# Norms by a power of -1/2 on POOL in place of ScalarE square roots and VectorE reciprocals: one step of an RWKV-7 / attention backbone

## The chip, the core and the metric

The kernel runs on one NeuronCore of a Trainium2 chip. The metric is the device time of one execution, in microseconds. The engines are named as in the profile: PE (TensorE), DVE (VectorE), ACT (ScalarE), POOL (GpSimd) and SP (SyncE, which issues all the DMAs here).

## The reference

One inference step of a model of two layers, for 256 context tokens and 1024 latent tokens of width 1024, all in float32. Layer 0 is bidirectional RWKV-7 time mixing beside a gated short convolution, layer 1 is grouped-query attention with 16 query and 4 key/value heads of 64. The norms are what matters for the change; there are five kinds:

```python
def rmsnorm(x, g):                       # rows of 1024 before each layer and at the end;
    xf = x.astype(f32)                   # heads of 64 for q and k
    y = xf * lax.rsqrt(jnp.mean(xf * xf, axis=-1, keepdims=True) + EPS)      # EPS = 1e-6
    return (y * g.astype(f32)).astype(x.dtype)

# layer 0, before the scan: keys to length one, per head of 64
kk = kk / jnp.maximum(jnp.sqrt(jnp.sum(kk * kk, axis=-1, keepdims=True)), 1e-12)
S_f, y_f = rwkv_scan(S0[:, 0], r_h, w_h[:, :, 0], k_h[:, :, 0], v_h, kk, a_h[:, :, 0], False)
S_b, y_b = rwkv_scan(S0[:, 1], r_h, w_h[:, :, 1], k_h[:, :, 1], v_h, kk, a_h[:, :, 1], True)
y = y_f + y_b
# layer 0, after the scan: group norm per head of 64
var = jnp.mean(jnp.square(y - mean), axis=-1, keepdims=True)
y = ((y - mean) * lax.rsqrt(var + GN_EPS)).reshape(B, L, A_WIDTH) * lnx_g + lnx_b   # GN_EPS = 64e-5
```

## The kernel before

**Order of the work.** Every stage is written as Python generators that yield what they need next (an engine and tiles) and then emit instructions. The class `Loom` is a planner: `issued` (lines 256 to 303) keeps a modelled clock for each engine, with the prices of `COST` (line 39), 6.25 ns per column for a reciprocal, and 1.28 us whenever ScalarE goes from one group of `TABLES` (line 46) to another; `run` (from line 327) always lets go on the generator that this model says can start in time, by the ranks of `PRECEDENCE`. What is emitted stands in program order on each engine, so a changed price or a changed engine gives all later work a new order. `pick` gives some additions to POOL or DVE, whichever the model has free first. The model knows no contention between DVE and POOL.

**Stages.** Start (0 to 60 us): rows of x are read, squared and summed on ACT, normed (`norm_x`), transposed and modulated, while the adaLN weights stream in. Even layer (to about 1170 us): `fill` runs the input projection, three fp32r products for each tile (high and low halves, `whi`, `wlo`, split from `wraw`), into which the scan is woven: 20 chunks for each of four pairs of heads, with products into the PSUM banks `wk`, `iv`, `ch`, `py`, triangular inverses of many small DVE operations on `acc` and `tmp`, and state steps in which POOL multiplies `hv` by the decay into `hg` and DVE adds it to PE's `ch`. Then the output projection, `rsqrt_mean` for each block of rows and the transposes for layer 1 (to about 1306), the odd layer's projections with the per-head norms (to about 1520), attention (to about 2140), the last products with `to_y`, which norms a block of rows and stores it.

**The norms.** All are Sqrt on ACT and RECIPROCAL on DVE:

- `norm_k` (from line 709): 20 groups of 128x256. ACT squares into `sq` (one buffer, `bufs=1`), PE sums each head by a product with `ones2` into a `wk` bank, ACT takes the root out of the bank, DVE takes the maximum with 1e-12 and the reciprocal, and one DVE operation scales the keys; a store follows on SP.
- `close_groups` (from line 1239): 20 groups of 128x256 in `sqy` (one buffer), root with scale 1/64 and bias `GN_EPS`, reciprocal on DVE, product with `y` on POOL, two DVE operations with the gates, a store.
- `norm_x` (from line 1296): three calls with 4, 2 and 4 columns.
- `rsqrt_mean` (line 1747): one column, for each of ten blocks of rows in both layers.
- `normed_heads` (line 1839): 4 or 8 columns, 30 times.

Tanh and Exp are the functions used most on ACT; Silu runs twice at the start.

Of the kernel before, what the change touches and what calls it, by code (L numbers as in the profile page):

```python
# [12 lines left out]
ALU = mybir.AluOpType  # L13
# [26 lines left out]
BIAS = {"V": 0.3, "sum": 3.0}  # L40


WINDOW = 3.413


TABLES = {AF.Tanh: 0, AF.Exp: 0, AF.Sqrt: 1, AF.Silu: 2}

PRECEDENCE = (("loaded", -0.1), ("bonuses", 0), ("h0", 0.3), ("chained", 0), ("moved", 0.3), ("tailed0", 0),
              ("evac", -0.1), ("h1", 1.0), ("x", -0.1), ("interacted", 0), ("solved1", 0), ("solved", 0),
# [67 lines left out]
class Loom:  # L117
# [128 lines left out]
    def issued(self, e, name, a, k, r):  # L246
        if not self.on:
            return
        args = list(a) + list(k.values())
        aps = [x for x in args if isinstance(x, bass.AP)]  # L250
        outs = [k["out"]] if "out" in k else aps[:1]
        if k.get("accum_out") is not None:
            outs.append(k["accum_out"])
        ins = [x for x in aps if not any(x is o for o in outs)]
        n = (ins if name == "tensor_reduce" else outs)[0].free_size()
        if e == "T":
            group = None
            if name == "transpose":
                dur = 0.107
            else:  # L260
                dur = max(0.054, n * (1 if ins[0].dtype == F32R else 4) / 2400.0)
                if ins[0].dtype == F32R and ins[0].partition_size() == 64:

                    group = ("rows", ins[0].start_partition() if callable(ins[0].start_partition) else ins[0].start_partition)
                    if self.last is not None and group != self.last:
                        dur, group = 0.014, None
                elif ins[0].free_size() <= 64:
                    group = outs[0].start_partition() if callable(outs[0].start_partition) else outs[0].start_partition
                    if self.last is not None and group != self.last:
                        dur, group = 0.053, None  # L270
            self.last = group
        elif e == "V":
            dur = COST[e][0] + n * (6.25e-3 if name == "reciprocal" else COST[e][1])
            if isinstance(k.get("scalar"), bass.AP):
                dur += 0.065
        elif e == "S":
            dur = COST[e][0] + n * COST[e][1] + 0.14 * isinstance(k.get("scale"), bass.AP) \
                + 0.09 * isinstance(k.get("bias"), bass.AP)
            f = a[2] if len(a) > 2 else None
            if f in TABLES and TABLES[f] != self.table:  # L280
                self.table = TABLES[f]
                dur += 1.28
        elif e == "G":
            dur = COST[e][0] + n * COST[e][1]
        items = [self.item(x, False) for x in ins] + [self.item(x, True) for x in outs]
        start = max([self.clock[e]] + [self.free(e, x) for x in items])
        if e == "T":
            dur = self.paced(start, dur, P if ins[0].dtype == F32R else ins[0].partition_size())
        if e == "D":
            self.clock[e] = start + 0.475  # L290
            piece = min(x.ap[-1][1] if x.ap[-1][0] == 1 else 1 for x in outs + ins)
            self.moved = max(self.moved, start + 1.1) + outs[0].nbytes() / (360e3 if piece >= 128 else 180e3)
            end = self.moved + 0.86
        else:
            self.clock[e] = end = start + dur
        for x in items:
            self.note(e, x, end)
        self.tc.keep_in_program_order(r)
        self.trace.append((r.ins.name, start, end))
# [68 lines left out]
def hybrid_step(  # L368
# [31 lines left out]
    V.memset(ones2[0:64, 0:64], 1.0)  # L400
    V.memset(ones2[64:128, 64:128], 1.0)
    eps_t = const.tile([P, 2], F32, name="eps_t")
    V.memset(eps_t[:, 0:1], EPS)
    V.memset(eps_t[:, 1:2], GN_EPS)


    rows = {}
# [307 lines left out]
    def norm_k(p, b, f, done):  # L715

        t0, n, _ = BLK[b]
        for h in range(0, n, GRP):
            fh = f[:, h:h + GRP]
            yield "S", fh  # L720
            sq = ip.tile([P, GRP], F32, tag="sq", name="sq", bufs=1)
            S.activation(sq, fh, AF.Square, scale=col("k_k", p))
            yield "T", sq, wk_ps
            pt = wk_ps.take()
            T.matmul(pt[:, 0:GRP], ones2, sq, start=True, stop=True)
            yield "S", pt
            S.activation(sq, pt[:, 0:GRP], AF.Sqrt)
            wk_ps.release(pt)
            yield "V", sq
            V.tensor_scalar(out=sq, in0=sq, scalar1=1e-12, scalar2=None, op0=ALU.max)  # L730
            yield "V", sq, 1.7
            V.reciprocal(out=sq, in_=sq)
            yield "V", sq, Into(fh)
            V.scalar_tensor_tensor(out=fh, in0=fh, scalar=col("k_k", p), in1=sq, op0=ALU.mult, op1=ALU.mult)
            dma(out=sp[p][:, 1, t0 + h:t0 + h + GRP], in_=fh)
        done()
        if b == 1:
            passed[f"k{p}"] = True
# [502 lines left out]
    def close_groups(x, p, gs):  # L1241
        yield lambda: passed[f"g{p}"]
        sqs, side = [], []
        for t0, y in gs:
# [9 lines left out]
            iv_ps.release(pm)  # L1254
            yield "S", y
            sq = fin.tile([P, GRP], F32, tag="sqy", name="sqy", bufs=1)
            S.activation(sq, y, AF.Square)
            yield "T", sq, iv_ps
            pm = iv_ps.take()
            T.matmul(pm[:, 0:GRP], ones2, sq, start=True, stop=True)  # L1260
            yield "S", pm
            S.activation(sq, pm[:, 0:GRP], AF.Sqrt, scale=1.0 / C, bias=eps_t[:, 1:2])
            iv_ps.release(pm)
            yield "V", sq
            V.reciprocal(out=sq, in_=sq)
            yield "G", sq
            G.tensor_tensor(out=y, in0=y, in1=sq, op=ALU.mult)
            yield "V", y, bon
# [27 lines left out]
    def norm_x(i0, n):  # L1296
        for i in range(i0, i0 + n):
            yield "S", xts[i]
            t = ldp.tile([P, D], F32, tag="xq", name="xq")
            S.activation(t, xts[i], AF.Square, accum_out=ss[:, i:i + 1])  # L1300
        yield "S", ss
        S.activation(ss[:, i0:i0 + n], ss[:, i0:i0 + n], AF.Sqrt, scale=1.0 / D, bias=eps_t[:, 0:1])
        yield "V", ss
        V.reciprocal(out=ss[:, i0:i0 + n], in_=ss[:, i0:i0 + n])
        for i in range(i0, i0 + n):
            yield "V", ss, xts[i]
            V.tensor_scalar(out=xts[i], in0=xts[i], scalar1=ss[:, i:i + 1], scalar2=None, op0=ALU.mult)
# [330 lines left out]
    class Proj:  # L1638
# [90 lines left out]
        def evac(self, i, h, pt):  # L1729
# [10 lines left out]
            yield "G", og, x  # L1740
            G.tensor_tensor(out=x, in0=x, in1=og, op=ALU.add)
            yield "S", x
            S.activation(og, x, AF.Square, accum_out=sums[self.l][:, i, h:h + 1])
            R["og"].release(og)
            yield from self.sink(i, h, x)

    def rsqrt_mean(ss):

        yield "V", ss
        V.tensor_tensor(out=ss[:, 2:3], in0=ss[:, 0:1], in1=ss[:, 1:2], op=ALU.add)  # L1750
        yield "S", ss
        S.activation(ss[:, 2:3], ss[:, 2:3], AF.Sqrt, scale=1.0 / D, bias=eps_t[:, 0:1])
        yield "V", ss
        V.reciprocal(out=ss[:, 2:3], in_=ss[:, 2:3])

    def x1_rows(i):
        return x1_d[i * P:(i + 1) * P, :]
# [82 lines left out]
    def normed_heads(pt, nh, w, i, free, sink):  # L1840
# [3 lines left out]
        ta, ssh = R["ta"].take(), R["ssh"].take()  # L1844
        ss, t = ssh[:, 0:nh], ta[:, 0:n]
        t3 = t.rearrange("p (h d) -> p h d", d=C)
        S.activation(t, pt, AF.Square)
        yield "V", t
        V.tensor_reduce(out=ss, in_=t3, axis=AX.X, op=ALU.add)
        yield "S", ss  # L1850
        S.activation(ss, ss, AF.Sqrt, scale=1.0 / C, bias=eps_t[:, 0:1])
        yield "V", ss
        V.reciprocal(out=ss, in_=ss)
        yield "V", ss
        V.tensor_tensor(out=t3, in0=pt.rearrange("p (h d) -> p h d", d=C),
                        in1=ss.unsqueeze(2).broadcast_to([P, nh, C]), op=ALU.mult)
# [595 lines left out]
```

## Time and profile before

| what | value |
|---|---|
| runs shown, median (lowest to highest) | 2253.53 us (2251.32 to 2257.36), 3 runs |
| the profiled execution | 2253.86 us, its span 2252.2 us |
| mean granted TensorE clock of the profiled execution | 0.951 of full speed |
| busy: PE, DVE, ACT, POOL | 2052.1, 1471.9, 1052.1, 1012.0 us |
| table loads on ACT | 56, 71.8 us |

The page gives the busy time of each engine over the span, a strip of 40 slices, the chain of work that ended last and the costliest groups. The clock is the share of full speed (2.4 GHz) that the throttle granted; the other level is 1.2 GHz. Since a helper emits every instruction, all have line 145: the tiles tell them apart. A tile's name without its number is its buffer; `mm`, `wk`, `py`, `pv`, `ch` and `iv` are PSUM banks, all else is SBUF or, with `_d` or `_dram`, device memory.

### The profile page before, as it was taken

Reading aid. Unit: us, or ns where it says so; the run is one execution under the profiler, and the core shown is the slowest. Engines: PE = TensorE matmul, PEld = TensorE weight load, DVE = VectorE, ACT = ScalarE, POOL = GpSimd, SP = SyncE. Lnnn points to the kernel's source line nnn. Section 1 sums busy time; section 2 is a strip of 40 time slices with the busy share of each in tenths; the row PEclk is TensorE's granted clock in tenths of the full one; section 3 lists DMA queues with packets and bytes.
Section 4 is the critical chain, followed back from the end, with each engine's and each line's share of the span. In section 5 each row is a group of like instructions: output and inputs, shape, how many; then the busy total and the mean of one; then the engine's idle time right before and its main releaser. Section 6 shows DMA issues by size and latency. Waiting matters only on the chain.

```text
span 2252.2 us, 42921 instructions
## 1 busy us (share of the span) xinstructions
PE 2052.1 (91%) x15306; PEld 1411.7 (63%) x15306; DVE 1471.9 (65%) x3483; ACT 1052.1 (47%) x2476; POOL 1012.0 (45%) x1152
## 2 busy tenths in 40 slices
PE   4998889798988988998979999999999999999898
PEld 1486666576666666666657788888454545454487
DVE  2346878948888886868645733552877777775443
ACT  3446556645665556554435632221354444444422
POOL 2434344333344343333224321430487777888622
PEclk7999899999998999999889999999799999999899
DMA  7834344324433333342345633323321211102243
GB/s 271 305 98 131 98 105 131 85 68 114 102 97 103 99 96 101 85 111 54 86 153 185 206 111 88 99 87 107 82 53 48 60 42 38 43 28 71 58 131 108
DMA packets 337818, 232.86 MB, mean 103 GB/s; under 512 B 163890, under 2 KB 289860, under 8 KB 335556
## 3 DMA queue, kind: packets, MB, share of 16 engines
q1 hardware_dynamic: 337604, 230.12, 35.0%
q8 instruction: 120, 1.97, 0.4%
q14 instruction: 94, 0.77, 0.1%
HBM read 166.95 MB, written 57.75 MB: 100 GB/s over the span
## 4 chain that ended last, share of the span: by engine, by line
PE 39%; DVE 9%; DMA 5%; issue 3%; ACT 1%; POOL 1%; SPq 1%; DVEq 0%; POOLq 0%; ACTq 0%
PE mm L145 21%; PE pv L145 8%; PE wk L145 5%; PE py L145 4%; DVE mx L145 3%; DVE rz L145 1%; DVE zs L145 1%; DMA rz<-rz_d 1%; PE ch L145 1%; DVE tmp L145 1%; SPq L145 1%; DVE acc L145 1%; DMA rz_d<-rc 1%; DMA rc<-rz 0%; DVE hv L145 0%
## 5 line engine op out<-in xcount | busy, mean ns | idle before, releaser
L145 POOL TENSOR_TENSOR zs<-zs,pe 128x512 f32<-128x512 f32 x275 | 366.8, 1370 | 34.1 <-ACT pe L145 32.1
L145 PE MATMUL mm<-h_hi,whi 128*128 128x512 f32 (+1 forms) x816 | 336.5, 412 | 4.3 <-ACT whi L145 4.1
L145 PE MATMUL mm<-h_hi,wlo 128*128 128x512 f32 (+1 forms) x816 | 299.3, 367 | 8.1 <-DVE wlo L145 7.2
L145 PE MATMUL mm<-h_lo,whi 128*128 128x512 f32 (+1 forms) x816 | 298.7, 366 | 0.0
L145 POOL TENSOR_TENSOR wlo<-wraw,whi 128x128 fp32r<-128x128 f32 x228 | 111.4, 494 | 246.0 <-ACT whi L145 205.8
L145 PE MATMUL pv<-pe,v_sb 128*64 128x512 f32 (+1 forms) x832 | 200.4, 604 | 0.0
L145 PEld LDWEIGHTS mm<-h_hi,whi 128*128 128x128 f32 x816 | 159.9, 196 | 49.5 <-issue 12.2
L145 PEld LDWEIGHTS mm<-h_hi,wlo 128*128 128x128 f32 x816 | 160.1, 196 | 37.1 <-DVE wlo L145 10.0
L145 DVE TENSOR_TENSOR acc<-acc,tmp 128x60 f32<-128x60 f32 (+23 forms) x620 | 168.0, 273 | 20.8 <-issue 2.9
L145 PE MATMUL mm<-wts,omh 128*128 128x512 f32 x648 | 166.6, 410 | 7.6 <-ACT wts L145 4.0
L145 PEld LDWEIGHTS mm<-h_lo,whi 128*128 128x128 f32 x816 | 161.0, 197 | 14.4
L145 PE MATMUL mm<-wts,h_hi 128*128 128x512 f32 x480 | 151.1, 396 | 0.0
L145 POOL TENSOR_TENSOR hg<-hv,gc 64x128 f32<-64x128 f32 x152 | 65.1, 428 | 185.0 <-DVE hv L145 173.9
L145 PEld LDWEIGHTS mm<-wts,omh 128*128 128x128 f32 x648 | 122.9, 194 | 38.0 <-ACT wts L145 5.3
L145 ACT ACTIVATE whi<-wraw 128x128 fp32r<-128x128 f32 x272 | 80.2, 305 | 78.2 <-DMA wraw<-in_w_in_e_dram 40.3
L145 DVE TENSOR_REDUCE mx<-mm 128x1 f32<-128x512 f32 (+1 forms) x138 | 89.7, 660 | 36.7 <-PE py L145 12.6
L145 DVE SCALAR_TENSOR_TENSOR hv<-ch,gc,hg 64x64 f32<-64x64 f32 x288 | 81.3, 282 | 49.3 <-PE ch L145 42.2
L145 POOL TENSOR_TENSOR xr<-xr,og 128x512 f32<-128x512 f32 x40 | 54.6, 1364 | 128.4 <-DVE og L145 93.3
L145 PEld LDWEIGHTS pv<-pe,v_sb 128*64 128x64 f32 x832 | 51.6, 139 | 93.9 <-issue 82.3
L145 DVE TENSOR_REDUCE mx<-py 128x1 f32<-128x512 f32 (+1 forms) x138 | 89.6, 660 | 28.7 <-PE mm L145 13.0
L145 DVE TENSOR_TENSOR tmp<-acc,nra 128x31 f32<-128x31 f32 (+7 forms) x320 | 90.1, 282 | 27.4 <-DMA acc<-eye_d 17.7
L145 ACT ACTIVATE pe<-py 128x512 f32<-128x512 f32 (+1 forms) x139 | 79.1, 587 | 60.3 <-PE mm L145 20.3
(284 smaller groups left out, 5189.5 us busy)
## 6 DMA issues: line engine op xcount, KB each, us to landing
wraw<-in_w_in_e_dram SPq DMA_DIRECT2D x272, 64.0 KB
wada<-in_w_ada_dram SPq DMA_DIRECT2D x16, 1024.0 KB
inp<-rkv_d SPq DMA_DIRECT2D x40, 384.0 KB
om<-om_d SPq DMA_DIRECT2D x52, 256.0 KB
wraw<-in_w_in_o_dram SPq DMA_DIRECT2D x40, 256.0 KB
wada<-in_w_ada_dram SPq DMA_DIRECT2D x16, 512.0 KB
rkv_d<-nb SPq DMA_DIRECT2D x24, 256.0 KB
lor<-lora_d SPq DMA_DIRECT2D x40, 128.0 KB
```

Of the source, the lines that this page charges most:

```text
L145: r = f(*a, **k)
```

## The change

Where a norm is computed, the mean is now folded into the square (a scale on ACT's Square) or added before, the epsilon or the maximum is applied to the sum, and POOL raises it to the power -1/2 in one TENSOR_TENSOR, whose second input is a column of -0.5 broadcast over the tile. Sqrt is used nowhere any more. In `close_groups` ACT's pass out of PSUM stays, as an Identity with the bias; in `norm_k` DVE's maximum now reads PSUM. In `norm_x` and `normed_heads` DVE adds the epsilon; in `rsqrt_mean` the two halves and the epsilon are added in one instruction. The planner gets a price for a power, 8 ns per column on top of POOL's 2.1, and a table of two groups in place of three.

```diff
+POW = 8e-3
-TABLES = {AF.Tanh: 0, AF.Exp: 0, AF.Sqrt: 1, AF.Silu: 2}
+TABLES = {AF.Tanh: 0, AF.Exp: 0, AF.Silu: 1}
...
-            dur = COST[e][0] + n * COST[e][1]
+            dur = COST[e][0] + n * (COST[e][1] + POW * (k.get("op") == ALU.pow))
...
-    V.memset(eps_t[:, 0:1], EPS)
     V.memset(eps_t[:, 1:2], GN_EPS)
+    minus_half = eps_t[:, 0:1]
+    V.memset(minus_half, -0.5)
... norm_k
-            yield "S", pt
-            S.activation(sq, pt[:, 0:GRP], AF.Sqrt)
+            yield "V", pt
+            V.tensor_scalar(out=sq, in0=pt[:, 0:GRP], scalar1=1e-24, scalar2=None, op0=ALU.max)
             wk_ps.release(pt)
-            yield "V", sq
-            V.tensor_scalar(out=sq, in0=sq, scalar1=1e-12, scalar2=None, op0=ALU.max)
-            yield "V", sq, 1.7
-            V.reciprocal(out=sq, in_=sq)
+            yield "G", sq
+            G.tensor_tensor(out=sq, in0=sq, in1=minus_half.broadcast_to([P, GRP]), op=ALU.pow)
... close_groups
-            S.activation(sq, y, AF.Square)
+            S.activation(sq, y, AF.Square, scale=C ** -0.5)
...
-            S.activation(sq, pm[:, 0:GRP], AF.Sqrt, scale=1.0 / C, bias=eps_t[:, 1:2])
+            S.activation(sq, pm[:, 0:GRP], AF.Identity, bias=eps_t[:, 1:2])
             iv_ps.release(pm)
-            yield "V", sq
-            V.reciprocal(out=sq, in_=sq)
+            yield "G", sq
+            G.tensor_tensor(out=sq, in0=sq, in1=minus_half.broadcast_to([P, GRP]), op=ALU.pow)
... rsqrt_mean (norm_x and normed_heads alike, with n and nh columns)
-        V.tensor_tensor(out=ss[:, 2:3], in0=ss[:, 0:1], in1=ss[:, 1:2], op=ALU.add)
-        yield "S", ss
-        S.activation(ss[:, 2:3], ss[:, 2:3], AF.Sqrt, scale=1.0 / D, bias=eps_t[:, 0:1])
-        yield "V", ss
-        V.reciprocal(out=ss[:, 2:3], in_=ss[:, 2:3])
+        V.tensor_scalar(out=ss[:, 2:3], in0=ss[:, 0:1], scalar1=ss[:, 1:2], scalar2=EPS, op0=ALU.add, op1=ALU.add)
+        yield "G", ss
+        G.tensor_tensor(out=ss[:, 2:3], in0=ss[:, 2:3], in1=minus_half, op=ALU.pow)
```

## Rows read from the trace of the kernel before

**Rows 1.** the page's busy time by engine, with shares of the span and instructions

```profile
PE 2052.1 (91%) x15306; PEld 1411.7 (63%) x15306; DVE 1471.9 (65%) x3483; ACT 1052.1 (47%) x2476; POOL 1012.0 (45%) x1152
```

**Rows 2.** stretches: length, then PE, PEld, DVE, ACT, POOL busy, clock, DMA, GB/s

```profile
180.00:1170.00 990.00, 873.68 (x9165) 640.95 (x9164) 764.23 (x2225) 539.43 (x1418) 376.20 (x625) 0.94 0.38 100
1170.00:1306.00 136.00, 130.19 (x587) 103.08 (x587) 81.52 (x166) 79.70 (x176) 52.82 (x38) 0.98 0.59 185
1306.00:1520.00 214.00, 214.00 (x975) 174.60 (x974) 99.61 (x178) 57.08 (x124) 60.70 (x49) 1.00 0.31 93
1520.00:2140.00 620.00, 587.65 (x3429) 321.53 (x3428) 414.40 (x677) 269.08 (x531) 432.41 (x333) 0.95 0.21 57
2140.00:2253.00 113.00, 104.09 (x460) 85.86 (x458) 43.54 (x79) 28.59 (x68) 27.91 (x21) 0.98 0.36 119
```

**Rows 3.** PE's waits, 180 to 1170: us in total, times, longest us

```profile
PE ch L145 <- DVE hv L145: 19.7, 30, 2.8
...
PE wk L145 <- ACT sq L145: 11.0, 7, 4.9
...
PE mm L145 <- POOL wts L145: 1.4, 2, 0.9
...
PE iv L145 <- ACT w L145: 0.3, 1, 0.3
...
PE mm L145 <- DVE wts L145: 0.2, 1, 0.2
```

**Rows 4.** ACT's groups, 180 to 1170: count | busy us, mean ns | idle before

```profile
L145 ACT ACT_TABLE_LOAD x43 | 55.2, 1283 | 0.8
...
L145 ACT ACTIVATE sq<-wk 128x256 f32<-128x256 f32 x15 | 5.8, 384 | 2.1 <-PE wk L145 1.9
```

**Rows 5.** DVE's reciprocals of 256 columns, same view and stretch

```profile
L145 DVE RECIPROCAL sqy<-sqy 128x256 f32<-128x256 f32 x20 | 34.9, 1746 | 4.4 <-ACT sqy L145 4.4
...
L145 DVE RECIPROCAL sq<-sq 128x256 f32<-128x256 f32 x15 | 26.2, 1748 | 0.3
```

**Rows 6.** POOL's product after the group norm, same view and stretch

```profile
L145 POOL TENSOR_TENSOR y<-y,sqy 128x256 f32<-128x256 f32 x20 | 15.9, 793 | 66.0 <-DVE sqy L145 49.1 <-DVE acc L145 15.6 <-DVE tmp L145 1.1
```

**Rows 7.** timeline near 245 us: start us, us, what [idle before <- releaser]

```profile
241.50 0.18 DVE L145 TENSOR_TENSOR tmp<-acc,nra 128x31 f32<-128x31 f32 x1
...
241.63 2.04 POOL L145 TENSOR_TENSOR nb<-f_pad 128x512 f32<-128x512 f32 x2 [0.80 <-DVE wlo L145]
...
241.72 1.00 DVE L145 TENSOR_TENSOR acc<-acc,tmp 128x31 f32<-128x31 f32 x1
242.76 0.96 DVE L145 TENSOR_TENSOR tmp<-acc,nra 128x30 f32<-128x30 f32 x1
...
245.73 1.75 DVE L145 RECIPROCAL sq<-sq 128x256 f32<-128x256 f32 x1
...
247.52 0.48 DVE L145 SCALAR_TENSOR_TENSOR nb<-nb,par,sq 128x256 f32<-128x256 f32 x1
...
248.04 0.51 ACT L145 ACTIVATE sq<-nb,par 128x256 f32<-128x256 f32 x1 [4.61 <-DVE nb L145]
...
248.60 0.80 PE L145 MATMUL wk<-sq,ones 128*128 128x256 f32 x1 [4.95 <-ACT sq L145]
```

**Rows 8.** timeline of the start, ACT, DVE and PE

```profile
10.55 1.28 ACT L145 ACT_TABLE_LOAD   x1
11.84 0.30 ACT L145 ACTIVATE ss<-ss,eps_t 128x4 f32<-128x4 f32 x1
...
12.38 2.74 DVE L145 TENSOR_SCALAR xt<-xt,ss 128x1024 f32<-128x1024 f32 x4
...
19.09 4.54 PE L145 MATMUL wk<-wada,cond 128*32 128x512 f32 x24 [6.11 <-ACT cond L145]
```

**Rows 9.** tile sums: duration ns min/median/max, first and last start us

```profile
L145 ACT ACTIVATE sums<-sums,eps_t x20: 294/295/298, 1173.0 to 2247.1; 128x1 f32<-128x1 f32 x20
...
L145 DVE RECIPROCAL sums<-sums x20: 148/163/167, 1173.3 to 2247.5; 128x1 f32<-128x1 f32 x20
```

More of the change, by code (lines that the diff above doesn't have):

```diff
@@ L1299, in norm_x @@
             t = ldp.tile([P, D], F32, tag="xq", name="xq")
-            S.activation(t, xts[i], AF.Square, accum_out=ss[:, i:i + 1])
-        yield "S", ss
-        S.activation(ss[:, i0:i0 + n], ss[:, i0:i0 + n], AF.Sqrt, scale=1.0 / D, bias=eps_t[:, 0:1])
+            S.activation(t, xts[i], AF.Square, scale=D ** -0.5, accum_out=ss[:, i:i + 1])
         yield "V", ss
-        V.reciprocal(out=ss[:, i0:i0 + n], in_=ss[:, i0:i0 + n])
+        V.tensor_scalar(out=ss[:, i0:i0 + n], in0=ss[:, i0:i0 + n], scalar1=EPS, scalar2=None, op0=ALU.add)
+        yield "G", ss
+        G.tensor_tensor(out=ss[:, i0:i0 + n], in0=ss[:, i0:i0 + n], in1=minus_half.broadcast_to([P, n]), op=ALU.pow)
         for i in range(i0, i0 + n):
@@ L1742, in evac @@
             yield "S", x
-            S.activation(og, x, AF.Square, accum_out=sums[self.l][:, i, h:h + 1])
+            S.activation(og, x, AF.Square, scale=D ** -0.5, accum_out=sums[self.l][:, i, h:h + 1])
             R["og"].release(og)
@@ L1749, in rsqrt_mean @@
         yield "V", ss
-        V.tensor_tensor(out=ss[:, 2:3], in0=ss[:, 0:1], in1=ss[:, 1:2], op=ALU.add)
-        yield "S", ss
-        S.activation(ss[:, 2:3], ss[:, 2:3], AF.Sqrt, scale=1.0 / D, bias=eps_t[:, 0:1])
-        yield "V", ss
-        V.reciprocal(out=ss[:, 2:3], in_=ss[:, 2:3])
+        V.tensor_scalar(out=ss[:, 2:3], in0=ss[:, 0:1], scalar1=ss[:, 1:2], scalar2=EPS, op0=ALU.add, op1=ALU.add)
+        yield "G", ss
+        G.tensor_tensor(out=ss[:, 2:3], in0=ss[:, 2:3], in1=minus_half, op=ALU.pow)
     def x1_rows(i):
@@ L1846, in normed_heads @@
         t3 = t.rearrange("p (h d) -> p h d", d=C)
-        S.activation(t, pt, AF.Square)
+        S.activation(t, pt, AF.Square, scale=C ** -0.5)
         yield "V", t
         V.tensor_reduce(out=ss, in_=t3, axis=AX.X, op=ALU.add)
-        yield "S", ss
-        S.activation(ss, ss, AF.Sqrt, scale=1.0 / C, bias=eps_t[:, 0:1])
         yield "V", ss
-        V.reciprocal(out=ss, in_=ss)
+        V.tensor_scalar(out=ss, in0=ss, scalar1=EPS, scalar2=None, op0=ALU.add)
+        yield "G", ss
+        G.tensor_tensor(out=ss, in0=ss, in1=minus_half.broadcast_to([P, nh]), op=ALU.pow)
         yield "V", ss
```

## The prediction, made before the change was run

> **What bounds the kernel now.** I read the page's busy shares first: PE is busy 2052 of 2252 us [rows 1], DVE is the next at 1472. An average over stages says little, so I cut the span by stage [rows 2]. From 1306 to 1520 PE has no idle time at all (the projections of the odd layer, with the per-head norms); in 1170 to 1306 it lacks 6 us, in the attention 32 us and in the last products 9 us. In the long stage from 180 to 1170 us, the even layer, PE is busy 873.7 of 990 us and its granted clock averages 0.94 of full speed. That is where an edit of the other engines can move the end: 35 of the 40 large norms lie there. There DVE is busy 764 us (77%), ACT 539 (54%), POOL 376 (38%).
>
> What ends PE's idle time in that stage stands in the list of waits [rows 3]: the 16 rows that end with DVE add up to 49 us (from 19.7 down to 0.2), the 12 that end with ACT to 48 us (from 11.0 down to 0.3), POOL's two to 2.2 us. The page's chain of waits does not reach back through this stage, so I argue from the list of waits.
>
> The timeline of one such wait shows what lies behind it [rows 7]. A DVE operation with two SBUF inputs takes 0.18 us alone; started under a POOL addition it takes 1.00 and 0.96 us and ends as the POOL instruction ends. Then comes the reciprocal, 1.75 us, then the ACT square, which had been idle 4.61 us, then PE, idle 4.95 us. So ACT is often only the messenger: DVE was late, by its own reciprocal and by POOL's instructions. POOL's time is not free for DVE here.
>
> **The change part by part, even layer.** *ACT.* 43 table loads lie in this stage, 55.2 us at 1283 ns [rows 4]. Afterwards no function outside Tanh, Exp and those that run without a load of their own is left there, so one load at most remains: 42 x 1.283 = 53.9 us go. The 15 square roots of `norm_k`, 5.8 us [rows 4], move off ACT; the 20 of `close_groups` become an Identity of the same size and stay. Together 60 us of 539.
> The Trainium skill (ScalarE: Activation LUTs, What ACT_TABLE_LOAD costs) puts a switch at 2.66 us, 1283 ns of load and 1380 ns of drain. The trace confirms the first figure, and after the load shown in [rows 8] the square root starts without a further gap, so I count no drain; with it ACT would lose some 118 us and the wait term below would be -18 in place of -10.
>
> *DVE.* The 35 reciprocals go: 34.9 + 26.2 = 61 us [rows 5]. The maximum in `norm_k` stays and reads PSUM in place of SBUF: nothing either way by its length, but PE's bank `wk` is now freed by DVE, the busier engine, and no longer by ACT.
>
> *POOL.* It gets 35 powers of 128x256 here. The trace has no power. From below the nearest row is POOL's 128x256 product, 0.79 us [rows 6]. From above I know only of the reciprocal, which costs DVE 1.75 us for those columns; POOL as much dearer over its product as DVE's reciprocal is over its 0.48 us scaling [rows 7] would be 0.79 x 1.75/0.48 = 2.9 us, and nothing forbids twice the planner's price, 5.3 us. The planner prices it 0.15 + 256 x (0.0021 + 0.008) = 2.74 us. Its other prices meet the rows: product 0.69 against 0.79 [rows 6], reciprocal 1.67 against 1.75 [rows 5]. I take 2.74, so 35 x 2.74 = 96 us more on POOL.
>
> *What the powers do to DVE.* In the timeline DVE lost some 80% of the time of each POOL addition, but there it did nothing except two-input operations. It also reads PSUM and idles, so I take two thirds: 1.8 us per power, 63 us in the stage. That cancels the 61 us of reciprocals: DVE gains nothing, it is stopped where it used to divide. If POOL's power left DVE its interface, DVE would gain the 61 us.
>
> *What is queued behind a power.* On POOL: the products `hg` of the scan, which DVE and then PE's `ch` need, and the low halves of weights `wlo`. On DVE: the scaling of `norm_k` with the store behind it on SP's queue, and there the weight loads; and the single buffer `sq`, which the next square needs. The latency of one norm hardly changes: load, square root and reciprocal, 1.28 + 0.38 + 1.75 = 3.4 us without the maximum and the handovers, against 2.74.
>
> **The sum.** I let an engine's lateness grow as its busy time over its idle time; that is a choice, since no row prices a marginal microsecond. ACT: 539/451 = 1.20 becomes 479/511 = 0.94, so 48 us of waits lose 21%, -10 us. DVE: 764/226 = 3.38 unchanged, 0. POOL: 376/614 = 0.61 becomes 472/518 = 0.91, half as much again on its 2.2 us and on a fifth, as I put it, of the 19.7 us that `hv` ends and `hg` feeds, +3 us. Stage: -7 us.
>
> **The other stages.** *Start:* the load and the square root between the last sum of squares and the first scaling take 10.55 to 12.38 us [rows 8]; an addition like the reciprocal's 0.18, a power of 4 columns at 0.2 and two handovers make it about 0.5. PE's first product at 19.09 waits behind DVE's list, so -1.3 us reaches it; the price runs from -1.5 to +1 if POOL's queue holds something else first. *Rows to the odd layer (1170 to 1306):* a few loads and ten small square roots go, where PE is idle 6 us; -1. *Per-head norms:* ACT loses 30 small square roots, DVE swaps a reciprocal for an addition, POOL gets 30 powers of some 0.2 us; all hidden under a PE that is never idle [rows 2]. If that cover were gone, each would wait behind one POOL addition of 1 us [rows 7], 30 us in all, but the banks of `mm` that they hold have not made PE wait once. *Attention:* has none of these norms; only the planner's picks shift. *Tail:* 0.295 on ACT and 0.163 on DVE [rows 9] become a power of one column; 0, within half a microsecond.
> Total: -7 - 1.3 - 1 = about -9 to -10 us. The profiled execution took 2253.86 us for a span of 2252.2, and the median is 2253.53: 2253.5 - 10 = 2243.5 us.
>
> **The rivals.**
> (a) *The power leaves DVE running.* Then 61 us of DVE go: 703/287 = 2.45 in place of 3.38, 28% of 49 us, -13.5 more: 2230 us. For it: a power computes long on each element and may need the interface seldom. Against it: a DVE operation on a 128x31 tile stood to the end of POOL's addition [rows 7].
> (b) *The power is longer than priced and stops DVE and the scan: slower.* Its place is the even layer. At 4.5 us per power DVE is stopped 3.55 of them, 35 x (3.55 - 1.75) = 63 us more: 827/163 = 5.07, half as much again on 49 us, +24.5; POOL 533/457, +5; with ACT's -10 and the -2.3 elsewhere +17: 2270 us. At 5.3 us it is about +37. The point from which it decides: DVE must lose some 31 us for the ACT gain to be eaten, 0.9 us per power, so from about 3.6 us on there is no gain. For it: POOL's product is already twice the length of the same work on DVE. The Trainium skill (GPSIMD Engine Reference, Engine selection and Specifications) says elementwise work belongs on VectorE, GpSimd being some 2x slower with two inputs, and that the SBUF interfaces are shared with VectorE operations that have two SBUF inputs; by that rule this rival is the forecast, and the trace agrees on the sharing [rows 7].
> (c) *The loads were hidden anyway.* ACT is idle 46% of the stage and in [rows 7] waits for DVE. Then only start and rows remain: 2251 us.
> That the loads would stay, because two of the remaining functions need different tables, I give nothing of its own: in the stage there are 43 loads for 35 square roots, and a root with its return takes up to two.
>
> **How the numbers follow.** Chances: forecast 0.42, (a) 0.18, (b) 0.24, (c) 0.16. Every case carries some 8 us of scatter, since the planner orders all later work anew from the changed prices. A difference of 0.3%, 6.8 us, is about what a measurement of this kernel can tell from no change. Faster by more: most of the forecast (0.33), all of (a), 0.02 of (c): 0.53. Within: 0.09 of the forecast, 0.13 of (c), 0.02 of (b): 0.24. Slower: 0.22 of (b) and the rest of (c), 0.23. The range reaches below (a) by its scatter and to the middle of (b): 2222 to 2270; the forecast's own is 2234 to 2253.
>
> **What would show it.** Three or so table loads in the run; no reciprocal of 256 columns; powers of 2.3 to 3.3 us. DVE's two-input operations of 0.2 us stretched to over 2 us under a power say that it is stopped, as in the forecast; unstretched ones say (a). PE's idle time in the even layer near 107 us; ACT's share of it below 40, DVE's still near 49. Waits of POOL `y` and `hg`, and of DVE for POOL, above those of before, with PE idle over 130 us, say (b). It would be wrong altogether if the idle time after 1306 us changed by more than the shift of the planner, or if the powers were below 1.5 or above 5 us.

## The result

The changed kernel takes 3798.56 us (median of 4 runs, 3795.16 to 3810.04) where the kernel before took 2252.43 beside it: 1.687 times as long, 95% interval 1.682 to 1.692. The prediction was 2243.5 us, in a range up to 2270. The profiled execution took 3796.96 us for a span of 3795.2, at a mean granted clock of 0.768.

The page of the changed kernel, busy time by engine (against [rows 1]). PE does the same 15306 products, ACT and DVE do less, as was meant; POOL has 1663 us more:

```profile
PE 2138.7 (56%) x15306; PEld 1464.5 (39%) x15306; DVE 1433.3 (38%) x3484; ACT 962.5 (25%) x2350; POOL 2675.3 (70%) x1184
```

The same view as [rows 2], with the stages where they now lie: the even layer, the step to the odd layer, its projections, attention, the last products. Columns: length, then busy PE, PEld, DVE, ACT, POOL, clock, DMA share, GB/s.

```profile
180.00:2650.00 2470.00, 959.29 (x9276) 707.96 (x9277) 731.71 (x2240) 484.14 (x1381) 1957.71 (x625) 0.68 0.15 39
2650.00:2830.00 180.00, 157.12 (x631) 116.04 (x630) 96.57 (x185) 89.70 (x191) 64.85 (x51) 0.89 0.58 183
2830.00:3060.00 230.00, 222.68 (x998) 177.65 (x997) 101.84 (x186) 46.55 (x92) 98.78 (x76) 1.00 0.29 88
3060.00:3680.00 620.00, 583.29 (x3403) 316.26 (x3401) 415.41 (x675) 267.03 (x528) 431.50 (x332) 0.95 0.20 56
3680.00:3796.00 116.00, 107.14 (x472) 88.35 (x471) 41.56 (x69) 24.94 (x58) 32.88 (x31) 0.97 0.36 118
```

The even layer took 990 us and takes 2470; nearly all of the loss is there. PE is idle for 1511 us of it, and its granted clock fell from 0.94 to 0.68. Over the whole run the same products take 87 us longer than before (2138.7 against 2052.1). Behind the even layer the step to the odd layer takes 44 us longer and the projections 16; attention and the last products have their old length.

POOL's groups in the changed kernel: count | busy us, mean ns | idle before and its releaser.

```profile
L148 POOL TENSOR_TENSOR sq<-sq,eps_t 128x256 f32<-128x256 f32 x20 | 823.7, 41186 | 21.5 <-DVE sq L148 13.0 <-DVE tmp L148 8.1
L148 POOL TENSOR_TENSOR sqy<-sqy,eps_t 128x256 f32<-128x256 f32 x20 | 822.8, 41142 | 38.0 <-ACT sqy L148 24.8 <-DVE acc L148 7.5 <-ACT gc L148 3.4
...
L148 POOL TENSOR_TENSOR ssh<-ssh,eps_t 128x8 f32<-128x8 f32 x20 | 34.9, 1744 | 46.3 <-DVE ssh L148 46.3
...
L148 POOL TENSOR_TENSOR y<-y,sqy 128x256 f32<-128x256 f32 x20 | 14.5, 723 | 1.1
...
L148 POOL TENSOR_TENSOR ssh<-ssh,eps_t 128x4 f32<-128x4 f32 x10 | 10.1, 1008 | 62.7 <-DVE ssh L148 62.7
```

A power of 128x256 takes 41.2 us, 57 times the product of the same size (`y`) and 15 times the 2.74 us of the sum. 39 of the 40 large ones lie in this stretch (the first starts at 138 us): 39 x 41.16 = 1605 us, for a stage that grew by 1480. With them POOL is busy for 1958 of the 2470 us. So two thirds of the loss need no wait at all: POOL's own work there is 968 us longer than the 990 us that the whole stage took before. The rest, 512 us, is time in which POOL is idle and waits for others, as they wait for it.

Who waits for them stands in the lists of waits: total us, times, longest us. First PE's five longest rows (against [rows 3]), then DVE's two:

```profile
PE wk L148 <- ACT sq L148: 298.9, 9, 38.3
PE ch L148 <- ACT hv L148: 257.6, 17, 75.3
PE iv L148 <- ACT sqy L148: 187.1, 6, 38.8
PE iv L148 <- DVE s_out L148: 118.5, 3, 41.3
PE mm L148 <- POOL wlo L148: 105.1, 3, 37.9
```

```profile
DVE nb L148 <- POOL sq L148: 791.2, 20, 74.4
DVE y L148 <- POOL y L148: 591.6, 16, 38.6
```

In PE's list POOL comes only fifth, with `wlo`; the four longest rows name ACT and DVE. The timeline of one such wait shows that there they are messengers. Start us, us, engine and what, [idle before <- releaser]:

```profile
923.08 41.29 POOL L148 TENSOR_TENSOR sqy<-sqy,eps_t 128x256 f32<-128x256 f32 x1
964.34 41.11 POOL L148 TENSOR_TENSOR sq<-sq,eps_t 128x256 f32<-128x256 f32 x1
1005.43 0.94 POOL L148 TENSOR_TENSOR hg<-hv,gc 64x128 f32<-64x128 f32 x2
1005.49 0.62 DVE L148 SCALAR_TENSOR_TENSOR nb<-nb,par,sq 128x256 f32<-128x256 f32 x1 [74.38 <-POOL sq L148]
1005.85 0.27 ACT L148 ACTIVATE hv<-ch 64x128 f32<-64x128 f32 x1 [76.22 <-POOL hg L148]
...
1006.94 1.03 PE L148 MATMUL iv<-ident,vt 128*64 128x128 f32 x4 [74.06 <-DVE hv L148]
```

Two powers stand back to back on POOL. Behind them wait two `hg` of 0.47 us each. DVE's scaling `nb` waits 74 us for the second power, ACT's `hv` 76 us for `hg`; DVE's copy into `hv` stands behind `nb` in DVE's list, and PE, idle for 74 us, waits for that copy.

DVE is not stopped by a power itself. In the changed kernel's trace, under a power that runs from 1016.39 to 1057.52 us, its two-input operations keep their length (against 1.00 us under an addition in [rows 7]). Over the whole run the 312 two-input operations on `acc` and `tmp` that lie wholly under a large power take 231 ns on average, the 648 with POOL at rest 210, the 265 that run beside other POOL instructions alone 471; under a power only those that start in its first 0.6 us are longer (up to 0.69 us). No DVE instruction of the whole run takes over 1.9 us:

```profile
1016.39 41.13 POOL L148 TENSOR_TENSOR sqy<-sqy,eps_t 128x256 f32<-128x256 f32 x1 [0.68 <-ACT sqy L148]
...
1017.07 0.22 DVE L148 TENSOR_TENSOR acc<-acc,tmp 128x70 f32<-128x70 f32 x1
...
1017.34 0.22 DVE L148 TENSOR_TENSOR tmp<-acc,nrb 128x65 f32<-128x65 f32 x1
```

Of ACT's 56 table loads 3 are left, as forecast:

```profile
L148 ACT ACT_TABLE_LOAD x3 | 3.8, 1283 | 3.8 <-DMA eye_d<-eye 3.0 <-PEq L2439 0.8
```

### The profile page after: what moved, and what is told of

Its sections match the earlier page's. It is cut to its first block, busy times and chain, and to the rows that moved or that the text cites. A ratio compares the mean times of both kernels' runs of the same rounds, so it can differ in the third digit from the quotient of the medians.

```text
span 3795.2 us, 42867 instructions
## 1 busy us (share of the span) xinstructions
PE 2138.7 (56%) x15306; PEld 1464.5 (39%) x15306; DVE 1433.3 (38%) x3484; ACT 962.5 (25%) x2350; POOL 2675.3 (70%) x1184
## 5 line engine op out<-in xcount | busy, mean ns | idle before, releaser
L148 POOL TENSOR_TENSOR sqy<-sqy,eps_t 128x256 f32<-128x256 f32 x20 | 822.8, 41142 | 38.0 <-ACT sqy L148 24.8
L148 POOL TENSOR_TENSOR sq<-sq,eps_t 128x256 f32<-128x256 f32 x20 | 823.7, 41186 | 21.5 <-DVE sq L148 13.0
L148 PE MATMUL mm<-h_hi,wlo 128*128 128x512 f32 (+1 forms) x816 | 315.6, 387 | 216.5 <-POOL wlo L148 105.1
L148 PE MATMUL mm<-h_hi,whi 128*128 128x512 f32 (+1 forms) x816 | 361.4, 443 | 0.4 <-ACT whi L148 0.3
L148 DVE SCALAR_TENSOR_TENSOR nb<-nb,par,sq 128x256 f32<-128x256 f32 x20 | 17.1, 853 | 791.2 <-POOL sq L148 791.2
L148 POOL TENSOR_TENSOR wlo<-wraw,whi 128x128 fp32r<-128x128 f32 x172 | 83.0, 489 | 211.8 <-ACT whi L148 162.5
L148 PE MATMUL wk<-sq,ones 128*128 128x256 f32 x40 | 20.9, 621 | 336.7 <-ACT sq L148 298.9
L148 PE MATMUL ch<-hv,tbk 128*64 128x64 f32 x608 | 37.8, 252 | 257.8 <-ACT hv L148 257.6
L148 DVE TENSOR_TENSOR acc<-acc,tmp 128x66 f32<-128x66 f32 (+24 forms) x620 | 171.0, 277 | 17.1
L148 ACT ACTIVATE hv<-ch 64x128 f32<-64x128 f32 x156 | 42.2, 271 | 440.3 <-POOL hg L148 343.9
```

Of the source, the lines that this page charges most:

```text
L148: r = f(*a, **k)
```

## The experiments

The theory after the result: the price of the power alone, paid through POOL's in-order queue. Rivals: the planner was told a wrong price and made a bad order; other parts of the change cost too; or a cheaper form of the power exists. Two further questions: would the forecast have held at the price it assumed, and why not.

Each ratio is to runs of the kernel before on the same chip; its median went from 2252 to 2260 us between the sets, so ratios are compared, and 0.1% is 2.3 us. The kernels whose names begin with d, and noload_b, leave the large norms uncomputed; a constant bounds the values in their place.

| kernel | order of | us | ratio (95%) |
|---|---|---|---|
| d0: products for the large powers | the change | 2306.6 | 1.0226 (1.0194 to 1.0258) |
| d16: powers on 16 columns | the change | 2301.7 | 1.0201 (1.0163 to 1.0239) |
| d64: powers on 64 columns | the change | 2583.7 | 1.1427 (1.1397 to 1.1457) |
| priced: the real price told | its own | 3603.2 | 1.594 (1.588 to 1.600) |
| after_b: the change | the kernel before | 3803.4 | 1.686 (1.678 to 1.693) |
| small: powers for small norms only | its own | 2305.7 | 1.0225 (1.0192 to 1.0258) |
| before_s: the kernel before | small | 2288.0 | 1.0117 (1.0086 to 1.0147) |
| small_b | the kernel before | 2276.8 | 1.0072 (1.0044 to 1.0099) |
| d16_b | the kernel before | 2283.2 | 1.0103 (1.0071 to 1.0134) |
| d0_b | the kernel before | 2254.9 | 0.9987 (0.9961 to 1.0013) |
| d0h_b: d0_b, heads as before | the kernel before | 2242.1 | 0.9912 (0.9887 to 0.9938) |
| noload_b: large roots without loads | the kernel before | 2256.2 | 0.9985 (0.9964 to 1.0005) |
| ars_b: 1/sqrt on ACT | the kernel before | 2233.5 | 0.9881 (0.9857 to 0.9905) |
| ars | its own | 2284.0 | 1.0125 (1.0097 to 1.0153) |

### What a power costs

Probe: scratch operations behind the last work of the kernel before, one execution.

```diff
... tiles, constants and 8 products of 128x256 on POOL
+    G.tensor_tensor(out=pa, in0=pa, in1=pe[:, 0:1].broadcast_to([P, GRP]), op=ALU.pow)
+    for i in range(100):
+        V.tensor_tensor(out=pw, in0=pz if i % 2 else pv, in1=pv, op=ALU.mult)
+    G.tensor_tensor(out=pa, in0=pa, in1=pe, op=ALU.pow)
... powers of 8, 32, 64, 128 columns; of 64, 32, 16 partitions; with exponents 1.5 and 1
```

> The kernel before, with POOL operations on scratch tiles behind its last work, and 100 DVE products of two SBUF inputs 128x256 that start with them. POOL: 8 products 128x256, a power with the exponent broadcast from one column, one with a full tile of exponents, powers of 8, 32, 64 and 128 columns, of 64, 32 and 16 partitions with 256 columns, and with exponents 1.5 and 1. Theory (price per column, partitions side by side): 41 us for both forms of exponent and for every count of partitions and exponent; 1.6, 5.4, 10.4 and 20.5 us for the columns. Rival, the broadcast of the exponent (a stride of zero) makes it slow: the full tile is far below 41 us. Rival, the cost goes by elements: 20, 10 and 5 us for 64, 32 and 16 partitions. Rival, a short-cut for simple exponents: the last ones far below. DVE: some 0.3 us alone and under a power if the power leaves it running, over 1 us under a power if it stops it; stretched under the POOL products either way.

Measured, by POOL's groups behind the kernel's end (`x10` mixes 8 products and the two first powers; `xr,xr` are the exponents 1.5 and 1):

```profile
L145 POOL TENSOR_TENSOR xr<-xr 128x256 f32<-128x256 f32 x10 | 88.6, 8861 | 0.9 <-DVE xr L145 0.2
L145 POOL TENSOR_TENSOR xr<-xr,xr 128x256 f32<-128x256 f32 x2 | 82.5, 41232 | 0.2
L145 POOL TENSOR_TENSOR xr<-xr 32x256 f32<-32x256 f32 x1 | 41.2, 41236 | 0.0
L145 POOL TENSOR_TENSOR xr<-xr 64x256 f32<-64x256 f32 x1 | 41.2, 41221 | 0.1
L145 POOL TENSOR_TENSOR xr<-xr 16x256 f32<-16x256 f32 x1 | 41.2, 41217 | 0.1
L145 POOL TENSOR_TENSOR xr<-xr 128x128 f32<-128x128 f32 x1 | 20.8, 20781 | 0.1
L145 POOL TENSOR_TENSOR xr<-xr 128x64 f32<-128x64 f32 x1 | 10.5, 10546 | 0.1
...
L145 POOL TENSOR_TENSOR xr<-xr 128x32 f32<-128x32 f32 x1 | 5.4, 5427 | 0.1
L145 POOL TENSOR_TENSOR xr<-xr 128x8 f32<-128x8 f32 x1 | 1.6, 1639 | 0.1
```

All rivals fall: neither the broadcast (41.1 us, with a full tile of exponents 41.2), nor the exponent, nor fewer partitions change it. From 32 to 128 columns, (20781 - 5427) / 96 = 160 ns per column, and 0.3 to 0.4 us to start. The Trainium skill (GPSIMD Engine Reference, Specifications) gives GpSimd eight cores with 16 partitions each. The trace agrees: 16 partitions take as long as 128. DVE, 128x256 with two SBUF inputs, first inside a power (the one at 2411.84 to 2453.08, which works on 32 partitions only; none of the 100 ran under a power on 128 or beside the products), then with POOL at rest. For powers on 128 partitions the changed kernel's own trace, above, stands:

```profile
L145 DVE TENSOR_TENSOR xr<-xr 128x256 f32<-128x256 f32 x15 | 6.4, 425 | 0.5
...
L145 DVE TENSOR_TENSOR xr<-xr 128x256 f32<-128x256 f32 x66 | 28.1, 426 | 2.3
```

### How the time follows the price

d16 and d64 in the changed kernel's own order: the planner is told 2.74 us as there. d0 has a product in the place of the power.

```diff
... d16, in norm_k; close_groups alike; half is a column of 0.5
-            G.tensor_tensor(out=sq, in0=sq, in1=minus_half.broadcast_to([P, GRP]), op=ALU.pow)
+            G.tensor_tensor(out=sq[:, 0:16], in0=sq[:, 0:16], in1=half.broadcast_to([P, 16]), op=ALU.pow)
```

> The changed kernel with the 40 large powers replaced by POOL products of the same 128x256 shape (0.79 us in place of 41.1); the planner is still told 2.74 us, so every engine's instructions stand in the changed kernel's order. The large norms are not computed here (a constant bound keeps the numbers finite); the loads, roots and reciprocals are gone all the same. Theory (the price of the power alone, paid through POOL's in-order queue): the 1546 us go, and with DVE rid of 61 us and ACT of 60 us the time is 2230 us or so, by the working of rival (a), 2220 to 2245. Rival, the order made from a wrong price is bad in itself: a good part of the 1546 us stays, over 2400 us. Rival, loads and reciprocals were hidden anyway: 2247 to 2255 us.

> As before, order unchanged, but each large power is taken on 16 of its 256 columns only, the rest of the tile left as it is (the large norms are not computed): by the small powers of the changed kernel (1.74 us for 8 columns, 1.01 for 4) that is 0.38 + 16 x 0.157 = 2.9 us, close to the 2.74 us of the prediction. Theory (price alone): the prediction's own case is made real, and since DVE is not stopped under a power the time is that of rival (a), 2230 us, at most 15 us above the kernel with products. If the prediction's sum holds with DVE stopped two thirds of each power: 2243. Rival, the order is bad in itself: over 2400.

> The changed kernel, in its own order, with each large power on 64 of its 256 columns (the large norms are not computed): 10.4 us each by the measured price per column, where 16 columns (2.9 us) gave 2302 us and all 256 (41.1 us) 3799. Theory, POOL's list is on the path from the start: the time rises along that line, 0.98 us for each us of power, to 2302 + 40 x 7.5 x 0.98 = 2595 us. Rival, POOL's idle time takes up the first part (35 x 7.5 = 263 us more in the even layer, where POOL is idle some 540): 2310 to 2380 us, and the line is steep only later.

At about 0.67 us per operation the time is 2306.6, at 2.96 us 2301.7, at 10.58 us 2583.7, at 41.16 us 3798.6. From 0.67 to 2.96 us nothing is lost in this order: the two intervals overlap. From 2.96 to 10.58 us the kernel gives 282 us for 305 of POOL, 0.93; from there 1215 for 1223, 0.99. So between 2.96 and 10.58 us POOL's power is already on the path nearly microsecond for microsecond, although POOL in d64 is busy for only 740 of the 1255 us of the even layer:

```profile
180.00:1435.00 1255.00, 955.55 (x9219) 704.61 (x9220) 718.88 (x2230) 478.77 (x1368) 740.37 (x618) 0.84 0.29 76
```

740 us are less than the 990 that the stage took before, so here it is not the sum of POOL's work that lengthens it but what waits behind single powers. Its idle time does not take them up: the rival fell. `d0` and `d16` missed the other way: 2230 was expected and both are 2% slower than the kernel before. That is a second loss, without any long power.

priced has POW at 0.158, and nothing else:

> The changed kernel, and nothing changed in it except that the planner is told the real price of a power (0.158 us per column, so 40.5 us for a large one). It computes everything. If the wrong price made the loss, the planner moves POOL's other work to DVE and starts powers early: POOL needs 35 x 41.1 us of powers and some 400 to 520 us beside them in the even layer, which then ends at 2020 to 2150 at the earliest: 3150 to 3300 us. If the loss is the power's length itself on an in-order queue whatever the plan: 3600 to 3820 us.

3603 us: the right price gives back 195 of the 1546 us, so the wrong price has a share, an eighth. PE then waits most for ACT's `hv`:

```profile
PE ch L148 <- ACT hv L148: 693.2, 43, 39.2
```

Even told the price, this planner does not place the powers harmlessly. No run cut a power into shorter pieces or gave it to another engine.

### The order by itself

The second loss called for the order and the work to be separated. The sequence in which the planner lets the generators go on, its choices between DVE and POOL and its choice of PSUM banks were written down for one kernel and followed by another, where each replacement stands at the place of what it replaces. PE's and SP's lists are then the same, instruction by instruction.

```diff
-        while self.live:
-            now = self.clock["T"]
...
+        for i in ORDER[0]:
+            g = self.live[i]
+            g[1] = self.needed(next(g[0], None))
```

> The 40 large norms as in the kernel before (square root on ACT, reciprocal on DVE); only the small ones (rows, tile sums, heads: 53 with 1 to 8 columns) by powers. It computes everything. Theory: 20 x 1.74 + 10 x 1.01 us and a few more on POOL, some 55 us, lie in the projections, where PE is never idle, and replace small roots on ACT: 2245 to 2256, no difference that counts. Rival, each small power holds a bank of mm behind POOL's queue: 30 x 1 us late, 2270 to 2285 us.

> The kernel before with all its own work (square roots, loads, reciprocals; no power), but its steps issued in the order that the planner made for the kernel with small powers only; TensorE's and SP's lists are the same as there. It computes everything. Theory O (the 53 us of the runs with short powers come from the new order alone): 2295 to 2315 us. Rival P (the small powers themselves cost them): 2248 to 2258 us.

> The converse: small norms by powers, large ones as before, the steps issued in the order of the kernel before (each power and addition in the place of the root or reciprocal that it replaces). It computes everything. Theory O: 2245 to 2260 us. Rival P: 2290 to 2315 us.

Neither side alone was right, and all three missed their ranges. The kernel before loses 1.2% by the order of `small` with no power in it; the small powers lose 0.7% in the order of the kernel before; together 2.2%. What the order does is seen in PE's busy time. The page's lines of before_s, ars and ars_b, with [rows 1] for the kernel before:

```profile
PE 2082.2 (91%) x15306; PEld 1426.0 (62%) x15306; DVE 1480.9 (65%) x3514; ACT 1051.1 (46%) x2473; POOL 995.1 (43%) x1124
```

```profile
PE 2086.5 (91%) x15306; PEld 1426.6 (62%) x15306; DVE 1400.7 (61%) x3398; ACT 1051.8 (46%) x2473; POOL 992.5 (43%) x1128
```

```profile
PE 2039.5 (92%) x15306; PEld 1402.1 (63%) x15306; DVE 1393.8 (63%) x3371; ACT 1051.7 (47%) x2476; POOL 1011.7 (45%) x1152
```

The products are the same 15306, but in before_s they take 30 us longer than before (2082 against 2052); only 6 of the 36 us between the two spans are idle time. In ars they take 47 us longer than in ars_b. It is so throughout: in the order of the kernel before the products take 2040 to 2071 us (seven kernels), in the other orders 2082 to 2088 (before_s, small, d0, d16, ars), while PE's idle time is 185 to 222 us in the first and 206 to 220 in the second. Cut into slices of 20 us from 180 to 1300, the granted clock is below 0.8 in 3 slices of the kernel before, in 10 of before_s, 9 of small, 9 of ars, 3 of ars_b, but also in 8 of small_b, so the count says less than the sums. Two such slices of before_s with the one ahead of them, and a slice of the kernel before:

```profile
540.00:560.00 20.00, 19.08 (x242) 14.60 (x239) 16.15 (x53) 12.58 (x42) 4.29 (x8) 1.00 0.39 97
560.00:580.00 20.00, 13.43 (x113) 9.28 (x113) 18.50 (x49) 5.22 (x15) 11.39 (x17) 0.72 0.36 89
580.00:600.00 20.00, 17.51 (x219) 12.96 (x214) 12.93 (x50) 6.81 (x22) 1.60 (x4) 0.59 0.44 113
```

```profile
580.00:600.00 20.00, 16.36 (x225) 11.36 (x224) 15.43 (x59) 8.86 (x30) 5.08 (x13) 1.00 0.54 162
```

In before_s PE is idle for 6.6 of 20 us, the clock falls, and the next slice runs at a mean of 0.59, most of it at the lower of its two levels; in the kernel before a slice with 3.6 us of idle time keeps 1.00. There the wait is lost first and then the clock. That the other orders bunch their waits more, and so lose the clock more often, is a reading of such slices and not shown.

> The changed kernel with all its own work, the powers at 41.1 us, in the order of the kernel before. It computes everything. If the price alone makes the loss: 3780 to 3820 us, as in its own order. If the order of the changed kernel carries a good part of it: below 3700 us.

At the real price it doesn't matter which of these two orders is taken: 1.686 against 1.687. Neither was made for a power of that length; the order of priced was, and gives 1.594. So the long power makes the loss in any of the three, and an order made for it takes an eighth off.

### The terms of the sum, in an unchanged order

> All norms by powers, the large ones on 16 of 256 columns (2.9 us each, near the 2.74 us of the prediction; the large norms are not computed), in the order of the kernel before: only the work differs. This is the sum of the prediction by itself: 2243.5 us if its -10 holds; 2230 if a power that leaves DVE running gives DVE's 61 us back too; 2249 to 2254 if loads and reciprocals were hidden anyway; over 2260 if powers at places not planned for hold up POOL's hg and wlo.

> The same with the 40 large powers replaced by products of 128x256 (0.79 us; the large norms are not computed), in the order of the kernel before: loads, roots and reciprocals gone for almost nothing on POOL. The upper end of what the relief of ACT and DVE can bring: 2230 us by rival (a), 2243 with ACT's part alone, 2249 to 2254 if all was hidden. The distance to the kernel with 16 columns is the price of 35 x 2.1 us on POOL: 0 to 5 us by the prediction's working.

> In the order of the kernel before, the 40 large powers replaced by products (the large norms are not computed), and the per-head norms put back to square root and reciprocal; rows and tile sums stay by powers. If the 30 powers of the per-head norms cost the 18 us that separate the run with small powers in this order from the kernel before, and the relief of ACT and DVE in the even layer is worth 22 us: 18 us below the run with products and powers of the heads, about 2236 us. If the heads cost nothing: 2255 us.

d0h_b is 0.88% faster than the kernel before, some 20 us: the relief of ACT and DVE is real. Putting the 30 powers of the heads back in (d0_b) costs 0.75%, 17 us, give or take 8 since the two were run in different sets. Lengthening the 40 operations on POOL from 0.6 to 2.9 us (d16_b) costs another 1.16%, 26 us; in the order of the change the same step, from d0 to d16, cost nothing, so this price belongs to the order too. In PE's list from 180 to 1120 us of d16_b against d0_b the rows that grew most are ACT's `sq` (6.7 to 11.3 us), DVE's `y` (1.5 to 4.8) and POOL's `wlo` (3.3 to 6.4); those of `hv`, which `hg` feeds, grew by 1.3 only. The heads' loss is seen in the stretch from the first projection of the odd layer to the first product of attention, of the kernel before, d0h_b, small_b and d0_b (columns as in [rows 2]):

```profile
1345.80:1574.20 228.40, 227.10 (x1035) 184.69 (x1034) 97.02 (x178) 57.09 (x123) 53.28 (x45) 1.00 0.31 96
```

```profile
1333.60:1561.80 228.20, 227.07 (x1034) 184.70 (x1032) 97.03 (x178) 56.93 (x123) 53.28 (x45) 1.00 0.31 96
```

```profile
1358.50:1601.50 243.00, 231.82 (x1034) 184.77 (x1032) 99.80 (x178) 47.36 (x91) 95.61 (x75) 0.99 0.29 90
```

```profile
1333.10:1576.80 243.70, 233.15 (x1035) 185.79 (x1033) 99.32 (x178) 47.58 (x91) 96.03 (x75) 0.99 0.29 90
```

Without the heads' powers 228 us, with them 243. The waits of small_b in that stretch, DVE's and PE's:

```profile
DVE ta L221 <- POOL ssh L221: 45.9, 30, 1.8
```

```profile
PE mm L221 <- DVE ta L221: 5.0, 13, 1.2
```

DVE waits 30 times for the power and reads the PSUM bank `mm` only then; PE, idle for 1.3 us there before, waits for the bank. Of the 15 us 10 are idle time: 5.0 for `mm`, 3.1 more than before for the load of `qt` (4.4 against 1.3) and 1.7 for DVE's `kl`. The other 5 are products that take longer (231.8 against 227.1 us for the same number); why was not separated.

noload_b has an Identity of the same length for the large square roots, so no loads; DVE keeps its reciprocals.

```diff
-            S.activation(sq, pt[:, 0:GRP], AF.Sqrt)
+            S.activation(sq, pt[:, 0:GRP], AF.Identity)
... the maximum with 64 in place of 1e-12; close_groups: Identity alike
```

> The kernel before, in its own order, with an Identity of the same length in the place of the 40 large square roots on ACT (the large norms are not computed): the 43 table loads of the even layer go, 54 us of ACT, and nothing else; DVE keeps its reciprocals. By ACT's term of the prediction (-10 us): about 10 us below the kernel before, 2249 us. If the loads were hidden (rival c): no difference, 2257 to 2262 us.

No difference that counts: -0.15%, at most 8 us by the interval. 44 of the 56 loads are gone, all 43 of the even layer among them. From 180 to 1120 us the rows of PE's waits that end with ACT add up to 33.1 us where they were 40.8, and those that end with DVE to 50.6 where they were 46.2, those that end with a DMA to 8.4 where they were 6.5: most of what ACT gave back others took.

ars_b and ars have ACT's function for 1/sqrt in the place of its square root. The reciprocals and the maximum go; a bias of 1e-24 stands for the maximum, by which the pass of `norm_k` takes 473 ns in place of 383.

```diff
-            S.activation(sq, pt[:, 0:GRP], AF.Sqrt)
+            S.activation(sq, pt[:, 0:GRP], AF.Abs_reciprocal_sqrt, bias=eps_t[:, 2:3])
             wk_ps.release(pt)
-            yield "V", sq
-            V.tensor_scalar(out=sq, in0=sq, scalar1=1e-12, scalar2=None, op0=ALU.max)
-            yield "V", sq, 1.7
-            V.reciprocal(out=sq, in_=sq)
... the other norms alike, each with its own scale and bias
```

> The kernel before, in its own order, with ACT's function for one over the square root in the place of its square root: all reciprocals and maxima of the norms go from DVE (61 us in the even layer), no power, nothing new on POOL, ACT as before with its table loads. It computes everything. By the working of rival (a), DVE's 61 us alone are worth 13.5 us: 2240 to 2246 us. If the relief of the runs with products came from ACT's loads: 2253 to 2259 us.

> The kernel with one over the square root on ACT once more, now in the order that the planner makes for it itself. It computes everything. If any change of a step brings an order at the planner's mercy, as with the short powers (30 us between the kernel before in its own order and in another one): 2240 to 2270 us, above its time in the order of the kernel before. If the new order does no harm: 2225 to 2240 us.

ars_b is the fastest kernel of the study: 2233.5 us, 1.2% below the kernel before (0.95 to 1.43%), with all of its 56 loads. DVE is busy 78 us less (1393.8 against 1471.9). In its own order the same work takes 2284 us, 50 more, above both of its ranges: any changed step brings a new order, and the new orders tried here were all worse than that of the kernel before, except at the real price of the power (priced).

## Why the prediction was wrong

**The power (the step that failed).** "The planner prices it 0.15 + 256 x (0.0021 + 0.008) = 2.74 us ... I take 2.74." It takes 41.2. The upper bound, 5.3 us, was twice an unmeasured price and so no bound at all. The planner's other prices met rows because they had been seen in rows; the power had none in any trace, and that was the reason to leave the top open. The prediction named the case, "wrong altogether ... if the powers were below 1.5 or above 5 us", and worked out nothing above 5.3 us. With 41.2 in place of 2.74 POOL gets 39 x 38.4 = 1498 us more in the stage, which grew by 1480.

**DVE stopped by the power.** Wrong: 425 ns inside a power on 32 partitions, 426 with POOL at rest, and 231 against 210 ns for the operations on `acc` and `tmp` under the powers of the changed kernel. The 1.8 us per power was read from an addition, which stops DVE [rows 7]. The condition of rival (a) held.

**What is queued behind a power.** `hg`, the scaling behind `sq`, the weights' `wlo`: right. The rows of PE's waits that name `sq`, `hv` and `wlo` add up to 910 of the 1511 us of idle time. The price at the assumed length is open: "+3 us" for 35 powers of 2.74 us, where 40 operations grown from 0.6 to 2.9 us cost 26 in the order of the kernel before and nothing in that of the change. Nor did the 26 come by the row that the sum scaled up: `hv` grew by 1.3 us, the others by more (`sq`, `y`, `wlo`). A wait worked out from busy over idle time knows only the rows that were there before.

**ACT's -10 us.** Rival (c) was right for ACT: 55 us of loads gone, -3 us and not separable from zero. The waits that end with ACT did fall as forecast, by 19% where 21% was said (40.8 to 33.1 us); but PE then waited for DVE and DMAs instead. The prediction called ACT "often only the messenger" and still took its rows as if nothing stood behind them.

**DVE's 61 us.** Put at 0 because it was thought to be stopped as long as it had divided; where nothing stops it, ars_b gives 27 us (with the small reciprocals and the maxima), twice rival (a)'s 13.5.

**The start.** -1.3 us: the product with `wada` of [rows 8] starts at 18.4 us in place of 19.1, -0.7. The power of 4 columns takes 1.03 us there, not 0.2.

**Per-head norms.** "all hidden under a PE that is never idle": 15 to 17 us. The text gave the price if the cover were gone, 30 us, and kept the cover because the banks of `mm` "have not made PE wait once". A power of 1.0 or 1.7 us was assumed at 0.2, and it lies between two DVE operations while a bank is held.

**The order.** "some 8 us of scatter": by the ratios 22 to 55 us between the same work in its own order and in that of the kernel before, in four pairs (d16, d0, small, ars).

**Rival (b)** had the right engine, place and sign. It put 24.5 us on a stopped DVE and 5 on POOL's queue; in the run POOL's queue carries nearly all of it, and slower products 87 us. Its sum also let DVE stand for the whole of each microsecond above 2.74, where the forecast took two thirds. Taken together at the assumed price (d16), the change is 2.0% slower; so the sign would have been wrong even with powers of 2.9 us, by the order and the heads' powers, which the prediction priced at nothing or at scatter. The Trainium skill's rule that speaks against the change (GPSIMD Engine Reference, Engine selection: elementwise work belongs on VectorE, GpSimd being some 2x slower with two inputs) gave the right direction. Its factor is for additions, products and maxima; the power here takes 57 times POOL's own product.

## What to carry to other kernels

An operation that no trace shows has no upper price: measure one instance of it, for its columns, before it is counted 40 times, and give the open top a chance. Then ask two things of an engine that gets such work: whether the sum makes it the longest of the stage (1958 us of POOL here, in a stage of 990), and, below that, what waits behind a single instruction (from 2.96 to 10.58 us each further microsecond of a power cost 0.93, with POOL busy for 59% of the stage at the end). The wait shows under the name of another engine. Where a planner orders the work, compare a change in a fixed order first; here a new order alone moved the time of kernels with short operations by 1 to 2.4%, more than most of the terms.

## What the hardware showed beyond that

- A power on POOL costs about 160 ns per column and 0.3 to 0.4 us to start, the same for 16 to 128 partitions, a full or broadcast exponent, and exponents -0.5, 1 and 1.5.
- A power leaves DVE's two-input operations near their full speed (231 ns on average against 210 with POOL at rest), while POOL's other instructions stretch them (471 ns; [rows 7]): whether POOL holds up DVE depends on the instruction.
- ACT's function for 1/sqrt takes 473 ns for 128x256 with a bias out of PSUM, as its square root with a bias does (475), and asks for as many table loads (56).
